# Storing the stationary operands of two GEMM stages with hi and lo side by side, and on 64 bytes

## The chip, the cores and the metric

The kernel runs on one core of one Trainium2 chip. The metric is the device time of one execution in microseconds (us); the time before is the median of three runs. The profile is of one further execution, and its times count from the start of its span. TensorE is called PE, its weight loads PEld, VectorE DVE, ScalarE ACT, GpSimd POOL and SyncE SP. L70 means line 70 of the kernel.

## What is computed

One encoder layer over 256 tokens with a model width of 2048, in float32:

```
hn   = rmsnorm(x) ; proj = hn @ w_in                      # 2048 x 18432, nine parts of 2048
o_a  = head_rmsnorm(hgrn2_bidirectional(q, v, f, lb)) * silu(z_a)          # group A
o_b  = rmsnorm(b_gate * conv3(c_gate * h_b)) * silu(z_b)                   # group B
h    = x + concat([o_a, o_b]) @ w_out                     # 4096 x 2048
gate = sigmoid(h @ w_ple_gate)                            # 2048 x 2048
h    = h + (p @ w_ple) * gate                             # p: 256 wide
out  = rmsnorm(h)
```

The change touches what `o_a` and `h` are stored as between two GEMMs, and not what is computed.

## The kernel before

**Two-part numbers.** PE takes the rounded type `float32r`. Each GEMM operand is stored as a rounded part `hi` and a rest `lo = value - hi`, and each product is made of three: hi x hi, hi x lo and lo x hi. For the weights the class `Stream` does it: SP loads 1 MB into one of three `raw` tiles, ACT rounds it into half of an `spl` tile (L69), and DVE subtracts (L70), up to three halves ahead of their use.

**Stages.** Up to about 866 us the kernel multiplies `hn` by `w_in` (`gemm_in`, lines 284 to 288), with the HGRN2 and convolution work of ACT, DVE and POOL under it. The outputs of that stage are the mixed activations. `mixa` (group A, 16 heads) is written in `finish_pair`, one head at a time: two transposes of `ogz` into PSUM, then ACT writes hi (L360) and DVE lo (L361). `mixb` (group B) is written at L587 and L588.

Then comes the output projection, four blocks of 512 columns. `gemm_tok` (lines 621 to 633) runs over the rows of the weight in steps `kt` of 128, and for each of the two token tiles m of 128 tokens it issues three matmuls:

```
pe.matmul(acc[m], lhsT=lh, rhs=w[:, k, 0, :], ...)    # L630: hi x hi
pe.matmul(acc[m], lhsT=lh, rhs=w[:, k, 1, :], ...)    # L631: hi x lo
pe.matmul(acc[m], lhsT=ll, rhs=w[:, k, 0, :], ...)    # L632: lo x hi
```

The activation is the stationary operand (`lhsT`, 128 columns, loaded anew for every matmul), the weight the moving one, 512 or 256 columns wide. Per block, `pa` sums the 16 steps of `mixa` and `pb` those of `mixb`; DVE adds each into the residual `hh`. `h_transposed` (L635 to L644) is called two and three steps later, inside the next block: PE transposes four 128x128 pieces of `hh` into one PSUM bank, and one ACT copy (L643) and one DVE subtraction (L644), each over 512 elements per partition, write `ht`.

The last stage is the gate, in blocks of 512, 512, 512, 256 and 256 columns (`GCOLS`): `gemm_tok` with `ht` as the stationary operand into `pg`, with the small product of `pt` and `w_ple` (into `pp`) ahead of each 512 columns. ACT makes the sigmoid (L679), DVE multiplies and adds, and `finish(m)` scales by the final norm and stores. The last 256 columns are made for token tile 0 and then for 1, so that `finish(0)` lies under the matmuls of tile 1. `table` (L672) loads an activation table early by a one-column activation into `dummy`.

**Where things lie.** In each partition `mixa` and `mixb` hold `[k][s][t]`: for each 128 rows k, 256 tokens of hi and then 256 tokens of lo, 4 bytes each; `ht` and `pt` likewise. A stationary load reads 128 neighbouring floats. By the program's allocation `mixa` starts at byte 196576 of a partition and `mixb`, right below it, at 163808, both 32 bytes past a multiple of 64; `ht` starts at 95232 and `pt` at 146432, both multiples of 64, as do the five `spl` tiles. The tiles of pool `ap`, below `mixa` until group A is done, are 32 bytes past a multiple of 64 too. `rx`, `rb`, `rf` and `dummy` are four tiles of two floats, in 32 bytes each.

The order of the instructions on an engine is the tile framework's, which also sets the waits; `at`/`tick` place the transposes by steps of `gemm_tok`.

Of the kernel before, what the change touches and what calls it, by code (L numbers as in the profile page):

```python
# [8 lines left out]
F32 = mybir.dt.float32  # L9
F32R = mybir.dt.float32r  # L10
U32 = mybir.dt.uint32
AF = mybir.ActivationFunctionType
ALU = mybir.AluOpType
# [4 lines left out]
P = 128  # L18
D = 2048
T = 256  # L20
NKT = D // P
NH = 16
# [58 lines left out]
def tile_hymba_encoder(  # L81
# [15 lines left out]
    act, dve, pool, pe = nc.scalar, nc.vector, nc.gpsimd, nc.tensor  # L97
    out2 = out[0].rearrange("(m p) d -> p m d", p=P)

    const = ctx.enter_context(tc.tile_pool(name="const", bufs=1))  # L100
    rawp = ctx.enter_context(tc.tile_pool(name="rawp", bufs=3))
    splp = ctx.enter_context(tc.tile_pool(name="splp", bufs=5))
    xsp = ctx.enter_context(tc.tile_pool(name="xsp", bufs=1))
# [3 lines left out]
    xp = xctx.enter_context(tc.tile_pool(name="xp", bufs=1, side="left"))  # L107
    mctx = ExitStack()
    mixp = mctx.enter_context(tc.tile_pool(name="mixp", bufs=1, side="right"))
    mixa = mixp.tile([P, NH, 2, T], F32R, name="mixa")  # L110
    actx = ExitStack()
    ap_ = actx.enter_context(tc.tile_pool(name="ap", bufs=1, side="right"))

# [10 lines left out]
    oblocks = [sum((ws.add(w_out[j, h]) for h in range(8)), []) for j in range(4)]  # L124
    gblocks, pblocks = [], []
# [48 lines left out]
    for j in range(4):  # L174
        sgn = 1 if j < 2 else -1
        pool.affine_select(
            out=tri[:, j, :], in_=tri[:, j, :], compare_op=ALU.is_ge, fill=0.0, base=0,
# [34 lines left out]
    def at(dt, fn):  # L212
        pend.append((now[0] + dt, len(pend), fn))

    def tick():
        now[0] += 1
        due = sorted(e for e in pend if e[0] <= now[0])
        for e in due:
            pend.remove(e)
        for e in due:  # L220
            e[2]()
# [9 lines left out]
            in1=xs[:, kt, 0, :], op0=ALU.mult, op1=ALU.subtract,  # L231
        )

    rx = const.tile([P, 2], F32, name="rx")
    rbc = const.tile([P, T], F32, name="rbc")
    rbc2 = const.tile([P, T], F32, name="rbc2")
    ss8 = const.tile([P, 2, 4], F32, name="ss8")
# [301 lines left out]
    mixb = None  # L539
# [7 lines left out]
    for i in range(8):  # L547
# [9 lines left out]
        for m in range(2):  # L557
            ct = 2 * i + m
            dve.tensor_scalar(cg[:, m, :], u[:, m, 0:T], cvw[:, 0, ct : ct + 1], None, op0=ALU.mult)
            for j in (1, 2):  # L560
                dve.scalar_tensor_tensor(
                    out=cg[:, m, :], in0=u[:, m, j : j + T], scalar=cvw[:, j, ct : ct + 1],
                    in1=cg[:, m, :], op0=ALU.mult, op1=ALU.add,
# [10 lines left out]
        for m in range(2):  # L574
            ct = 2 * i + m
            dve.scalar_tensor_tensor(
                out=hb[:, m, :], in0=hb[:, m, :], scalar=cnw[:, ct : ct + 1], in1=sz[:, m, :],
# [3 lines left out]
        if i == 0:  # L581
# [3 lines left out]
            mixb = bp.tile([P, NH, 2, T], F32R, name="mixb")  # L585
        hi, lo = mixb[:, 2 * i : 2 * i + 2, 0, :], mixb[:, 2 * i : 2 * i + 2, 1, :]
        act.copy(out=hi, in_=cg)  # L587
        dve.tensor_tensor(out=lo, in0=cg, in1=hi, op=ALU.subtract)  # L588

    rb = const.tile([P, 2], F32, name="rb")  # L590

    def norm_b():
        rp = psm.tile([P, 512], F32, tag="kv", name="rp")
# [16 lines left out]
    hp = ctx.enter_context(tc.tile_pool(name="hp", bufs=1, side="left", reuse_waits="tile"))  # L610
    hh = hp.tile([P, 2, D], F32, name="hh")
    nc.sync.dma_start(hh, xtok)
    ht = xsp.tile([P, NKT, 2, T], F32R, tag="act", name="ht")

    pr = hp.tile([P, 2, T], F32, name="pr")
    nc.sync.dma_start(pr, pt_in)
    pt = hp.tile([P, 2, 2, T], F32R, name="pt")
# [3 lines left out]
    def gemm_tok(acc, ids, lhs, n, ms=(0, 1)):  # L621

        kp = 1024 // n
        nk = len(ids) * kp
        for kt in range(nk):
            w = ws.get(ids[kt // kp])
            k = kt % kp
            for m in ms:
                lh, ll = lhs(kt, 0)[:, m * P : (m + 1) * P], lhs(kt, 1)[:, m * P : (m + 1) * P]
                pe.matmul(acc[m], lhsT=lh, rhs=w[:, k, 0, :], start=(kt == 0), stop=False)  # L630
                pe.matmul(acc[m], lhsT=lh, rhs=w[:, k, 1, :], start=False, stop=False)  # L631
                pe.matmul(acc[m], lhsT=ll, rhs=w[:, k, 0, :], start=False, stop=(kt == nk - 1))  # L632
            tick()

    def h_transposed(j, kk):  # L635
        tp = psm.tile([P, 512], F32, tag="tr" if kk == 0 else "kv", name=f"ht{j}_{kk}")
        for k in range(2):
            kt = 4 * j + 2 * kk + k
            for m in range(2):
                pe.transpose(tp[:, k * T + m * P : k * T + (m + 1) * P], hh[:, m, kt * P : (kt + 1) * P], ident)  # L640
        kt = 4 * j + 2 * kk
        tpv = tp.rearrange("p (k t) -> p k t", k=2)
        act.copy(out=ht[:, kt : kt + 2, 0, :], in_=tpv)  # L643
        dve.tensor_tensor(out=ht[:, kt : kt + 2, 1, :], in0=tpv, in1=ht[:, kt : kt + 2, 0, :], op=ALU.subtract)  # L644

    for j in range(4):
        cs = slice(512 * j, 512 * (j + 1))
        pa = [psg.tile([P, 512], F32, tag="g", name=f"pa{j}_{m}") for m in range(2)]
        gemm_tok(pa, oblocks[j][:8], lambda kt, s: mixa[:, kt, s, :], 512)
        for m in range(2):  # L650
            dve.tensor_tensor(out=hh[:, m, cs], in0=pa[m], in1=hh[:, m, cs], op=ALU.add)
        pb = [psg.tile([P, 512], F32, tag="g", name=f"pb{j}_{m}") for m in range(2)]
        gemm_tok(pb, oblocks[j][8:], lambda kt, s: mixb[:, kt, s, :], 512)
        for m in range(2):
            dve.scalar_tensor_tensor(
                out=hh[:, m, cs], in0=pb[m], scalar=rb[:, m : m + 1], in1=hh[:, m, cs], op0=ALU.mult, op1=ALU.add
            )
        for kk in range(2):
            at(2 + kk, lambda j=j, kk=kk: h_transposed(j, kk))
# [4 lines left out]
    fw = gp.tile([P, D], F32, name="fw")  # L664
    nc.sync.dma_start(fw, final_norm_w.rearrange("(o d) -> o d", o=1).broadcast_to([P, D]))
    ssf = const.tile([P, 2, 5], F32, name="ssf")
    rf = const.tile([P, 2], F32, name="rf")
    dummy = const.tile([P, 2], F32, name="dummy")

    def table(func, j):  # L670

# [2 lines left out]
    def gated(j, m, cs, pg, pl, last):  # L674

        n = cs.stop - cs.start
        gt = gp.tile([P, 512], F32, tag="gt", name=f"gt{j}_{m}", bufs=2)
        h = hh[:, m, cs]
        act.activation(gt[:, :n], pg, AF.Sigmoid)  # L679
        if last:  # L680
            table(AF.Sqrt, 0)
        dve.tensor_tensor(out=gt[:, :n], in0=gt[:, :n], in1=pl, op=ALU.mult)
        dve.tensor_tensor(out=h, in0=gt[:, :n], in1=h, op=ALU.add)
        if last:
            dve.scalar_tensor_tensor(
                out=gt[:, :n], in0=h, scalar=1.0, in1=h, op0=ALU.mult, op1=ALU.mult,
                accum_out=ssf[:, m, j : j + 1],
            )
        else:
            act.activation(gt[:, :n], h, AF.Square, accum_out=ssf[:, m, j : j + 1])  # L690
        pool.tensor_tensor(out=h, in0=h, in1=fw[:, cs], op=ALU.mult)  # L691

    def finish(m):
        r = rf[:, m : m + 1]
        dve.tensor_reduce(out=r, in_=ssf[:, m, :], op=ALU.add, axis=AX.X)
        act.activation(r, r, AF.Sqrt, bias=epst, scale=1.0 / D)
        if m == 0:
            table(AF.Sigmoid, 1)
        dve.reciprocal(out=r, in_=r)
        c0 = 0  # L700
        for q, n in enumerate((256, 512, 768, 512)):
            cs = slice(c0, c0 + n)
            c0 += n
            if q % 2 == 0 or m == 0:
                dve.tensor_scalar(hh[:, m, cs], hh[:, m, cs], r, None, op0=ALU.mult)
            else:
                act.mul(hh[:, m, cs], hh[:, m, cs], r)
            nc.sync.dma_start(out2[:, m, cs], hh[:, m, cs])

    for j, (c0, n) in enumerate(GCOLS):  # L710
        cs = slice(c0, c0 + n)
        if c0 % 512 == 0:
            pp = [psm.tile([P, 512], F32, tag=("o", "sc")[m], name=f"pp{j}_{m}") for m in range(2)]
            gemm_tok(pp, pblocks[c0 // 512], lambda kt, s: pt[:, kt, s, :], 512)
            pl = []
            for m in range(2):
                t = gp.tile([P, 512], F32, tag="pl", name=f"pl{j}_{m}", bufs=4)
                act.copy(out=t, in_=pp[m])
                pl.append(t)
        pg = [psg.tile([P, 512], F32, tag="g", name=f"pg{j}_{m}")[:, :n] for m in range(2)]  # L720
        po = slice(c0 % 512, c0 % 512 + n)
        if j < len(GCOLS) - 1:
            gemm_tok(pg, gblocks[j], lambda kt, s: ht[:, kt, s, :], n)
            for m in range(2):
                gated(j, m, cs, pg[m], pl[m][:, po], False)
        else:
            for m in range(2):
                gemm_tok(pg, gblocks[j], lambda kt, s: ht[:, kt, s, :], n, (m,))
                gated(j, m, cs, pg[m], pl[m][:, po], True)
                finish(m)  # L730

# [55 lines left out]
```

## Time and profile before

| | us |
|---|---|
| median of 3 runs | 1158.66 (1158.42 to 1159.83) |
| the profiled execution | 1158.74 |
| its span | 1157.0 |
| PE busy, weight loads busy | 1142.3, 981.4 |
| DVE, ACT, POOL busy | 763.6, 639.9, 234.8 |
| output projection, first matmul | at 866.3 |
| gate, first matmul of `pg` | at 1051.3 |

The span is the profiled window; the rest of the execution's time lies around it. Busy times of PE overlap from one matmul to the next, since a matmul's time runs on while the next one streams: the cost of a matmul in a row is the distance from its start to the next start, which the timeline shows, and not its duration.

### The profile page before, as it was taken

The page shows a single profiled execution, that of the slowest core. Times are in us where ns is not written, and L with a number is a line of the kernel's source. Part 1 is how long each engine was busy: PE and PEld are TensorE (multiplying, and loading weights), DVE is VectorE, ACT ScalarE, POOL GpSimd, SP SyncE. Part 2 cuts the span into 40 slices and gives each one's busy share as a digit, 9 for nine tenths or more (in the row PEclk, how much of TensorE's full clock was granted, in tenths as well). Part 3 has the DMA queues.
Part 4 walks back from the last instruction along what each step waited for, and adds up shares of the span by engine and source line. Part 5 has one row for each costly group of instructions (what it writes and reads, how often), then busy time and mean ns, then how long its engine had stood idle before and what let it go on. Part 6 is the DMA issues. An engine that isn't in the chain of part 4 may idle for free.

```text
span 1157.0 us, 16851 instructions
## 1 busy us (share of the span) xinstructions
PE 1142.3 (99%) x6832; PEld 981.4 (85%) x6832; DVE 763.6 (66%) x949; ACT 639.9 (55%) x889; POOL 234.8 (20%) x167
## 2 busy tenths in 40 slices
PE   8999999999999999999999999999999999999997
PEld 7878888888888888888888888888888888888886
DVE  6687777685958585966666666676666545545554
ACT  6767576666758584855544444444444334434554
POOL 1232414151414041331221221121210000000121
PEclk9999999999999999999999999999999999999999
DMA  8754545454544555455555555555557555555541
GB/s 284 301 175 153 183 163 196 152 183 146 198 167 159 174 177 181 152 178 182 183 187 184 198 191 187 182 182 184 187 190 262 183 198 180 191 204 196 197 166 74
DMA packets 31614, 214.29 MB, mean 185 GB/s; under 512 B 3504, under 2 KB 3888, under 8 KB 7088
## 3 DMA queue, kind: packets, MB, share of 16 engines
q1 hardware_dynamic: 31392, 213.14, 53.6%
q8 instruction: 53, 0.87, 0.3%
q14 instruction: 25, 0.20, 0.1%
q10 hardware_dynamic: 144, 0.08, 0.0%
HBM read 211.11 MB, written 2.10 MB: 184 GB/s over the span
## 4 chain that ended last, share of the span: by engine, by line
PE 93%; DVE 2%; DMA 2%; POOL 1%; ACT 1%; SPq 0%; issue 0%; ACTq 0%; DVEq 0%
PE a L288 41%; PE a L287 21%; PE a L284 3%; PE pa L630 3%; PE pb L630 3%; PE pb L631 3%; PE pb L632 3%; PE pa L631 3%; PE pa L632 3%; PE pg L630 3%; PE pg L631 3%; PE pg L632 3%; PE a L285 1%; DVE spl L70 1%; PE scps L459 1%; PE cx L501 1%
## 5 line engine op out<-in xcount | busy, mean ns | idle before, releaser
L70 DVE TENSOR_TENSOR spl<-raw,spl 128x1024 fp32r<-128x1024 f32 (+1 forms) x389 | 522.3, 1348 | 305.9 <-ACT spl L69 304.9
L288 PE MATMUL a<-xs,spl 128*128 128x512 f32 x1680 | 597.2, 398 | 0.0
L69 ACT CAST spl<-raw 128x1024 fp32r<-128x1024 f32 (+1 forms) x389 | 405.0, 1045 | 343.0 <-PE a L288 193.7
L287 PE MATMUL a<-xs,spl 128*128 128x256 f32 x1680 | 476.0, 283 | 0.5 <-DVE spl L70 0.3
L288 PEld LDWEIGHTS a<-xs,spl 128*128 128x128 f32 x1680 | 316.7, 189 | 73.0
L287 PEld LDWEIGHTS a<-xs,spl 128*128 128x128 f32 x1680 | 318.1, 189 | 3.7 <-DVE spl L70 1.3
L288 PE MATMUL a<-spl,xs 128*128 128x512 f32 x480 | 171.4, 401 | 2.2 <-DVE spl L70 2.2
L287 PE MATMUL a<-spl,xs 128*128 128x256 f32 x480 | 135.4, 282 | 0.0
L288 PEld LDWEIGHTS a<-spl,xs 128*128 128x128 f32 x480 | 91.0, 190 | 24.1 <-DVE spl L70 2.5
L287 PEld LDWEIGHTS a<-spl,xs 128*128 128x128 f32 x480 | 91.4, 190 | 0.7
L307 ACT COPY r<-a 128x256 f32<-128x256 f32 x112 | 40.6, 372 | 47.4 <-PE a L288 46.8
L691 POOL TENSOR_TENSOR hh<-hh,fw 128x512 f32<-128x512 f32 (+1 forms) x10 | 12.8, 1293 | 264.5 <-PE pp L632 245.0
L630 PE MATMUL pg<-spl,ht 128*128 128x512 f32 (+1 forms) x160 | 55.7, 348 | 0.0
L632 PE MATMUL pg<-spl,ht 128*128 128x512 f32 (+1 forms) x160 | 55.5, 347 | 0.0
L631 PE MATMUL pg<-spl,ht 128*128 128x512 f32 (+1 forms) x160 | 55.5, 347 | 0.0
L630 PE MATMUL pa<-spl,mixa 128*128 128x512 f32 x128 | 51.2, 400 | 0.0
L438 POOL TENSOR_TENSOR qc<-pf,ge 128x256 f32<-128x256 f32 x16 | 43.9, 2748 | 34.4 <-DVE pf L430 34.4
L631 PE MATMUL pb<-spl,mixb 128*128 128x512 f32 x128 | 50.6, 395 | 0.0
L630 PE MATMUL pb<-spl,mixb 128*128 128x512 f32 x128 | 50.6, 395 | 0.0
L632 PE MATMUL pb<-spl,mixb 128*128 128x512 f32 x128 | 50.6, 395 | 0.0
L631 PE MATMUL pa<-spl,mixa 128*128 128x512 f32 x128 | 50.6, 395 | 0.0
L632 PE MATMUL pa<-spl,mixa 128*128 128x512 f32 x128 | 50.6, 395 | 0.0
(174 smaller groups left out, 1233.7 us busy)
## 6 DMA issues: line engine op xcount, KB each, us to landing
raw<-in_w_in_dram SPq DMA_DIRECT2D x140, 1024.0 KB, 5.0
raw<-in_w_out_dram SPq DMA_DIRECT2D x32, 1024.0 KB, 4.9
raw<-in_w_gate_dram SPq DMA_DIRECT2D x12, 1024.0 KB, 4.9
raw<-in_w_gate_end_dram SPq DMA_DIRECT2D x4, 1024.0 KB, 4.9
raw<-in_w_in_dram SPq DMA_DIRECT2D x7, 512.0 KB, 8.4
xf<-in_xtok_dram SPq DMA_DIRECT2D x1, 2048.0 KB, 9.9
hh<-in_xtok_dram SPq DMA_DIRECT2D x1, 2048.0 KB, 8.8
raw<-in_w_ple_dram SPq DMA_DIRECT2D x4, 512.0 KB, 3.5
```

What stands on the lines that cost most here:

```text
L69: self.nc.scalar.copy(out=v[:, :, 0, :], in_=r)
L70: self.nc.vector.tensor_tensor(out=v[:, :, 1, :], in0=r, in1=v[:, :, 0, :], op=ALU.subtract)
L284: pe.matmul(a, lhsT=lh, rhs=rf, start=True, stop=False)
L285: pe.matmul(a[:, :T], lhsT=ll, rhs=rh, start=False, stop=False)
L287: pe.matmul(a[:, :T], lhsT=ll, rhs=rh, start=False, stop=False)
L288: pe.matmul(a, lhsT=lh, rhs=rf, start=False, stop=(kt == NKT - 1))
L307: act.copy(out=r, in_=acc[m][:, 1, :])
L438: pool.tensor_tensor(out=c64(dst[:, d]), in0=c64(src[:, d, :, half * P : (half + 1) * P]), in1=g.unsqueeze(3).broadcast_to([P, 2, 2, CH]), ...
L630: pe.matmul(acc[m], lhsT=lh, rhs=w[:, k, 0, :], start=(kt == 0), stop=False)
L631: pe.matmul(acc[m], lhsT=lh, rhs=w[:, k, 1, :], start=False, stop=False)
L632: pe.matmul(acc[m], lhsT=ll, rhs=w[:, k, 0, :], start=False, stop=(kt == nk - 1))
L691: pool.tensor_tensor(out=h, in0=h, in1=fw[:, cs], op=ALU.mult)
```

## The change

Four edits, and new views of the tiles in the calls of `gemm_tok`:

- `mixa` is allocated with 8 more floats per partition (32 bytes) at its end, and its view becomes `[k][t][s]`: hi and lo of one token lie side by side. The parts that ACT and DVE write and that PE loads now step by 8 bytes.
- `ht` becomes two halves. In the first (kt 0 to 7) the order is `[k][m][t][s]`, a step of 8 bytes; in the second (kt 8 to 15) it is `[k][t][m][s]`: hi and lo of token t of tile 0, then of token t of tile 1, a step of 16 bytes.
- `h_transposed` writes `ht` with one ACT copy and one DVE subtraction for each 128 rows, of 256 elements each, where it had one of each for two.
- `rx`, `rb`, `rf` and `dummy` become views of one tile `few` of 16 floats.

`mixb`, `pt` and the weights keep their order. Pools on the right side are stacked from the top down, so the longer `mixa` moves its own start, `mixb` and the tiles of `ap` 32 bytes down.

```diff
-    mixa = mixp.tile([P, NH, 2, T], F32R, name="mixa")
+    mixa = mixp.tile([P, NH * 2 * T + 8], F32R, name="mixa")[:, : NH * 2 * T]
+    mixa = mixa.rearrange("p (k t s) -> p k s t", k=NH, s=2)
...
-    rx = const.tile([P, 2], F32, name="rx")
+    few = const.tile([P, 16], F32, name="few")
+    rx, rb, rf, dummy = (few[:, 2 * j : 2 * j + 2] for j in range(4))
...
-    ht = xsp.tile([P, NKT, 2, T], F32R, tag="act", name="ht")
+    htt = xsp.tile([P, NKT * 2 * T], F32R, tag="act", name="ht")
+    htv = [htt[:, : NKT * T].rearrange("p (k m t s) -> p k s m t", k=NKT // 2, m=2, s=2),
+           htt[:, NKT * T :].rearrange("p (k t m s) -> p k s m t", k=NKT // 2, m=2, s=2)]
+    def ht(kt, s, m):
+        return htv[kt // 8][:, kt % 8, s, m, :]
...
-                lh, ll = lhs(kt, 0)[:, m * P : (m + 1) * P], lhs(kt, 1)[:, m * P : (m + 1) * P]
+                lh, ll = lhs(kt, 0, m), lhs(kt, 1, m)
...
-        tpv = tp.rearrange("p (k t) -> p k t", k=2)
-        act.copy(out=ht[:, kt : kt + 2, 0, :], in_=tpv)
-        dve.tensor_tensor(out=ht[:, kt : kt + 2, 1, :], in0=tpv, in1=ht[:, kt : kt + 2, 0, :], op=ALU.subtract)
+        for k in range(2):
+            tpv = tp[:, k * T : (k + 1) * T].rearrange("p (m t) -> p m t", m=2)
+            hi, lo = (htv[(kt + k) // 8][:, (kt + k) % 8, s] for s in range(2))
+            act.copy(out=hi, in_=tpv)
+            dve.tensor_tensor(out=lo, in0=tpv, in1=hi, op=ALU.subtract)
```

More of the change, by code (lines that the diff above doesn't have):

```diff
@@ L588, in tile_hymba_encoder @@
         dve.tensor_tensor(out=lo, in0=cg, in1=hi, op=ALU.subtract)
-    rb = const.tile([P, 2], F32, name="rb")
     def norm_b():
@@ L648, in tile_hymba_encoder @@
         pa = [psg.tile([P, 512], F32, tag="g", name=f"pa{j}_{m}") for m in range(2)]
-        gemm_tok(pa, oblocks[j][:8], lambda kt, s: mixa[:, kt, s, :], 512)
+        gemm_tok(pa, oblocks[j][:8], lambda kt, s, m: mixa[:, kt, s, m * P : (m + 1) * P], 512)
         for m in range(2):
@@ L652, in tile_hymba_encoder @@
         pb = [psg.tile([P, 512], F32, tag="g", name=f"pb{j}_{m}") for m in range(2)]
-        gemm_tok(pb, oblocks[j][8:], lambda kt, s: mixb[:, kt, s, :], 512)
+        gemm_tok(pb, oblocks[j][8:], lambda kt, s, m: mixb[:, kt, s, m * P : (m + 1) * P], 512)
         for m in range(2):
@@ L666, in tile_hymba_encoder @@
     ssf = const.tile([P, 2, 5], F32, name="ssf")
-    rf = const.tile([P, 2], F32, name="rf")
-    dummy = const.tile([P, 2], F32, name="dummy")
     def table(func, j):
@@ L713, in tile_hymba_encoder @@
             pp = [psm.tile([P, 512], F32, tag=("o", "sc")[m], name=f"pp{j}_{m}") for m in range(2)]
-            gemm_tok(pp, pblocks[c0 // 512], lambda kt, s: pt[:, kt, s, :], 512)
+            gemm_tok(pp, pblocks[c0 // 512], lambda kt, s, m: pt[:, kt, s, m * P : (m + 1) * P], 512)
             pl = []
@@ L722, in tile_hymba_encoder @@
         if j < len(GCOLS) - 1:
-            gemm_tok(pg, gblocks[j], lambda kt, s: ht[:, kt, s, :], n)
+            gemm_tok(pg, gblocks[j], ht, n)
             for m in range(2):
@@ L727, in tile_hymba_encoder @@
             for m in range(2):
-                gemm_tok(pg, gblocks[j], lambda kt, s: ht[:, kt, s, :], n, (m,))
+                gemm_tok(pg, gblocks[j], ht, n, (m,))
                 gated(j, m, cs, pg[m], pl[m][:, po], True)
```

## The prediction

> **What bounds the kernel.** I read the page, then the busy times of the two stages that use the changed tiles, then the groups by line and shape, and then the timeline of PE inside these stages.
>
> ```profile
> span 1157.0 us, 16851 instructions
> PE 1142.3 (99%) x6832; PEld 981.4 (85%) x6832; DVE 763.6 (66%) x949; ACT 639.9 (55%) x889; POOL 234.8 (20%) x167
> PE 93%; DVE 2%; DMA 2%; POOL 1%; ACT 1%; SPq 0%; issue 0%; ACTq 0%; DVEq 0%
> ```
>
> The chain that ended last is PE for 93%. In the windows of the two stages (columns: PE, PEld, DVE, ACT and POOL busy, granted clock, DMA share, GB/s):
>
> ```profile
> 866.00:1051.00 185.00, 185.00 (x810) 149.07 (x810) 98.16 (x97) 76.49 (x79) 3.59 (x2) 1.00 0.59 203
> 1054.00:1148.00 94.00, 94.00 (x506) 81.72 (x505) 51.82 (x58) 46.67 (x66) 12.05 (x9) 1.00 0.44 150
> ```
>
> PE never stops from 866 to 1148 us, at the full granted clock; DVE works about half of it, ACT and the DMAs less. So the time of these 282 us is the number of matmuls times the distance from one start to the next. The changed tiles are stationary operands of exactly these matmuls. The groups:
>
> ```profile
> L630 PE MATMUL pa<-spl,mixa 128*128 128x512 f32 x128 | 51.2, 400 | 0.0
> L631 PE MATMUL pb<-spl,mixb 128*128 128x512 f32 x128 | 50.6, 395 | 0.0
> L630 PE MATMUL pg<-spl,ht 128*128 128x512 f32 x96 | 37.6, 391 | 0.0
> L631 PE MATMUL pg<-spl,ht 128*128 128x256 f32 x64 | 18.1, 283 | 0.0
> L630 PE MATMUL pp<-spl,pt 128*128 128x512 f32 x16 | 6.2, 389 | 0.0
> ```
>
> Three lines share each group's count: 384 matmuls on `mixa`, 384 on `mixb`, 288 of 512 columns and 192 of 256 on `ht`. The same shape takes longer on `mixa` and `mixb` than on `ht` and `pt`. The timeline gives the distances (first and last of a row of matmuls: start, duration, line):
>
> ```profile
> 883.69 0.40 PE L632 MATMUL pa<-spl,mixa 128*128 128x512 f32 x1
> ...
> 886.49 0.40 PE L632 MATMUL pa<-spl,mixa 128*128 128x512 f32 x1
> ```
> ```profile
> 904.69 0.40 PE L632 MATMUL pb<-spl,mixb 128*128 128x512 f32 x1
> ...
> 908.89 0.40 PE L632 MATMUL pb<-spl,mixb 128*128 128x512 f32 x1
> ```
> ```profile
> 1119.65 0.39 PE L632 MATMUL pg<-spl,ht 128*128 128x512 f32 x1
> ...
> 1122.37 0.39 PE L632 MATMUL pg<-spl,ht 128*128 128x512 f32 x1
> ```
> ```profile
> 1129.75 0.28 PE L631 MATMUL pg<-spl,ht 128*128 128x256 f32 x1
> ...
> 1131.43 0.28 PE L630 MATMUL pg<-spl,ht 128*128 128x256 f32 x1
> ```
>
> `mixa`: 12 steps in 2.80 us, 233.3 ns each. `mixb`: 18 in 4.20, 233.3. `ht`: 12 in 2.72, 226.7, and at 256 columns 14 in 1.68, 120.0. From the last two, 256 columns stream in 106.7 ns, so 512 take 213.3, and each matmul carries a surcharge of 13.3 ns whatever its width; on `mixa` and `mixb` it is 20.0. The moving operand is `spl` in all four, the PSUM banks of `pa`, `pb` and `pg` are the same, and `pp` uses others at the pace of `pg`. What differs is the stationary tile: `mixa` and `mixb` start 32 bytes past a multiple of 64, `ht` and `pt` on one.
>
> **Part 1, the placing.** 32 bytes more in `mixa` put its start at 196576 - 32 = 196544 and `mixb`'s at 163776, both multiples of 64, and every piece in them starts a multiple of 512 or 1024 bytes further (lo in `mixa` 4 bytes past that, inside the same 64). If the 6.7 ns come from the offset, all 768 matmuls of the output projection lose them: 768 x 6.7 = 5.1 us. They lie on PE's unbroken row, so the end moves by all of it. What would be late next are the splits of the weights; with DVE at half its time they have room.
>
> **Part 2, the strided loads.** `mixa` and the first half of `ht` are loaded with a step of 8 bytes (384, and 144 + 96 matmuls), the second half of `ht` with 16 (144 + 96). Before has no strided load, so this is bounded from both sides.
>
> ```profile
> 1052.76 0.60 PE L640 MATMUL ht<-ident,hh 128*128 128x128 f32 x4
> ```
> ```profile
> L640 PE MATMUL ht<-ident,hh 128*128 128x128 f32 x32 | 4.8, 272 | 0.0
> ```
> ```profile
> L631 PEld LDWEIGHTS pa<-spl,mixa 128*128 128x128 f32 x128 | 24.0, 188 | 5.5
> L631 PEld LDWEIGHTS pg<-spl,ht 128*128 128x128 f32 x160 | 30.3, 190 | 3.6
> ```
>
> In the four transposes the streams are short and the loads set the pace: (0.60 - 0.27) / 3 = 0.109 us per load. That leaves a load 0.118 us of slack under 512 columns and 0.011 under 256. The load's own row is no longer off the 64 bytes (188 against 190), so what the offset costs is paid by the stream, not by the load. From below: the surcharge of all 864 strided matmuls could vanish, 864 x 13.3 = 11.5 us less. From above: a load that reads each element from a place of its own could take two or more times 0.109, or disturb the stream in proportion to the bytes it passes over; the rivals price both. I take zero: the nearest rows, loads of 128 elements with a dense step, are hidden at both widths.
>
> The Trainium skill, page SBUF — State Buffer, section Specifications, states that SBUF has 16-byte lines, that a read needs at least two hits on a line for full bandwidth, and that each crossing to a new line costs. By it the step of 8 bytes (two floats of a line) is free and the step of 16 (one) is not, which speaks against the second half of `ht`; no row of before has such a load, and the third case below is what it would do here.
>
> **Part 3, the writes.**
>
> ```profile
> L643 ACT CAST ht<-ht 128x512 fp32r<-128x512 f32 x8 | 4.7, 587 | 2.4 <-PE ht L640 2.4
> L644 DVE TENSOR_TENSOR ht<-ht,ht 128x512 fp32r<-128x512 f32 x8 | 5.5, 689 | 1.5 <-ACT ht L643 1.5
> L307 ACT COPY r<-a 128x256 f32<-128x256 f32 x112 | 40.6, 372 | 47.4 <-PE a L288 46.8
> L308 DVE TENSOR_TENSOR hb<-a,r 128x256 f32<-128x256 f32 x48 | 18.5, 423 | 13.8 <-ACT r L307 13.8
> L360 ACT ACTIVATE mixa<-ogt,vec 128x256 fp32r<-128x256 f32 x16 | 7.5, 469 | 0.0
> L361 DVE SCALAR_TENSOR_TENSOR mixa<-ogt,vec,mixa 128x256 fp32r<-128x256 f32 x16 | 7.6, 478 | 0.0
> ```
>
> The 8 copies and 8 subtractions of `ht` become 16 of half the length: ACT 16 x 372 - 8 x 587 = 1.3 us more, DVE 16 x 423 - 8 x 689 = 1.3 us more, in 185 us in which DVE is free for 87. The last four pieces are the ones that could be late: their transposes end at 1053.4, and kt 12 of the gate's first block comes 72 matmuls of 226.7 ns, 16 us, after the block's start at 1051.3. That covers four operations of under 0.5 us, and would cover them at double length. Without that cover the last chain of four would cost 0.8 us. The 16 + 16 writes of `mixa` keep their number; if a step of 8 bytes doubled them, ACT and DVE would each have 7.6 us more, spread over eight pairs under `gemm_in`. I put that at zero, with 1 us as the upper bound, since DVE is busy for 474 of 660 us there:
>
> ```profile
> 40.00:700.00 660.00, 657.31 (x4369) 572.46 (x4368) 474.00 (x612) 409.29 (x594) 183.99 (x115) 1.00 0.52 177
> ```
>
> **Part 4, one tile for four.**
>
> ```profile
> 1150.30 0.20 ACT L672 ACTIVATE dummy<-epst 128x1 f32<-128x1 f32 x1
> 1150.41 0.16 DVE L695 TENSOR_REDUCE rf<-ssf 128x1 f32<-128x5 f32 x1
> ```
>
> If the framework takes `few` as one thing, the reduction into `rf` must wait for the activation into `dummy`, which ends at 1150.50. Behind it on DVE stands the reciprocal, and the last stores wait for that: 0.1 to 0.2 us at the end. In `finish(0)` the reciprocal would wait 1.5 us for the next table, under the matmuls of tile 1. Zero to 0.2 us; I take 0.
>
> **The sum** against the profiled execution: 1158.74 - 5.1 = 1153.6. The median of the runs shown is 0.08 lower, so 1153.5.
>
> **The rivals.**
> *The strided loads disturb the stream less.* The surcharge depends on how the load's bytes lie (13.3 against 20.0 ns), so another pattern can also lower it. Against it: no row shows less than 13.3 in these stages. At half the surcharge 864 x 6.7 = 5.8 us more is gained, 1147.8; at none, 1142.0.
> The Trainium skill, page TensorE: Matmul & The Clock Gate, section Back-to-back issue gap, gives N / 2.4 + 2.5 ns for a single matmul, 215.8 at 512 columns; the trace shows 226.7, so the measurement decides for dense loads, and by the page's figure as an estimate the strided stages would end near 1144.
>
> *Slower: loads with a step of 16 bytes set the pace at 256 columns.* Place: the 96 matmuls of kt 8 to 15 in the last two blocks. A load twice as long takes 0.218 us, hidden under 226.7 at 512 columns but not under 120.0: 96 x 0.098 = 9.4 us, 1162.9. It decides from 0.120 + 5.1 / 96 = 0.173 us per load on. For it: only 0.011 us of slack there. Against it: nothing shows that a load's time depends on its step.
>
> *Slower: the surcharge grows with the bytes passed over*, 1024 and 2048 in place of 512: 26.7 and 53.3 ns. `mixa` gains nothing and loses 384 x 6.7 = 2.6 us, `mixb` gains 2.6, `ht` loses 240 x 13.3 + 240 x 40 = 12.8: 1171.5. For it: an offset of 32 bytes alone costs half as much again. Against it: one more piece in nine should cost a ninth, not a half.
>
> *The change doesn't do what it says:* the 6.7 ns belong to the place of `mixa` and `mixb` at the top of the memory, not to 64 bytes, and strides cost nothing: 1158.7.
>
> **How the numbers follow.** Forecast 0.34; less disturbance 0.26; long loads 0.16; bytes passed over 0.15; no effect 0.09. The first two are faster, 0.60; the next two slower, 0.31; the last the same, 0.09. 0.2% is 2.3 us, about what a measurement of this kernel can tell from no change. The range goes from the second case's end, 1142, over the long loads to half of the fourth case (surcharges grown half as far, 1165) with the 1 and 0.2 us of parts 3 and 4 and a little for loads over twice as long: 1167. It leaves out most of the fourth case. For the faster cases alone it is 1142 to 1156.
>
> **What would show it.** Right: in the profile after, distances of 226.7 ns on `mixa` and `mixb`, with 226.7 and 120.0 on `ht` in both halves, the gate as long as before and the projection 5 us shorter. Wrong: 233 on `mixb` (the offset isn't the cause); distances on `mixa` or `ht` below 220 (second case); about 0.2 us at 256 columns for kt 8 to 15 alone, with longer PEld rows there (third); distances that grow by step, 240 and 267, at both widths (fourth). DVE or ACT as a releaser of PE after 866 us would say that part 3 was mispriced.

## The result and the profile after

| | before | after |
|---|---|---|
| median, us | 1159.24 (4 runs) | 1167.69 (4 runs) |
| ratio to before | | 1.0072, 95% interval 1.0059 to 1.0084 |
| profiled span, us | 1157.0 | 1165.5 |

The kernel became slower by 8.4 us, where 5.1 us less were forecast. One execution of a kernel below, the profiled one of e2, took 1879.19 us at a granted clock of 0.556; it does not count in that kernel's ratio, and its profile is not used. The page of after, first lines and chain:

```profile
span 1165.5 us, 16875 instructions
PE 1151.2 (99%) x6832; PEld 1001.9 (86%) x6832; DVE 767.6 (66%) x957; ACT 643.2 (55%) x897; POOL 234.9 (20%) x167
PE 93%; DVE 2%; DMA 2%; POOL 1%; ACT 1%; issue 0%; SPq 0%; ACTq 0%; DVEq 0%
```

PE is still the chain, and no wait of PE is recorded from 866 us to the end of its matmuls. The span grew by 8.5 us and the busy time of PEld by 20.5. The groups by line and shape of after (busy us, mean ns; L639 to L641 are before's L630 to L632):

```profile
L640 PE MATMUL pa<-spl,mixa 128*128 128x512 f32 x128 | 50.4, 394 | 0.0
L640 PE MATMUL pb<-spl,mixb 128*128 128x512 f32 x128 | 49.8, 389 | 0.0
L640 PEld LDWEIGHTS pg<-spl,ht 128*128 128x128 f32 x160 | 41.0, 256 | 1.8
L640 PE MATMUL pg<-spl,ht 128*128 128x512 f32 x96 | 38.0, 396 | 0.0
L640 PEld LDWEIGHTS pa<-spl,mixa 128*128 128x128 f32 x128 | 24.7, 193 | 4.9
L640 PEld LDWEIGHTS pb<-spl,mixb 128*128 128x128 f32 x128 | 24.0, 188 | 5.1
L640 PE MATMUL pg<-spl,ht 128*128 128x256 f32 x64 | 21.7, 340 | 0.0
```

The loads of `ht` went from 190 to 256 ns on average, those of `mixa` from 188 to 193. The timeline of PE in after: `mixa`, `mixb`, the last two gate blocks' kt 0 to 7, and their kt 8 to 15 (first and last of 16, 20, 17 and 15 matmuls in a row):

```profile
879.76 0.39 PE L640 MATMUL pa<-spl,mixa 128*128 128x512 f32 x1
...
883.26 0.39 PE L640 MATMUL pa<-spl,mixa 128*128 128x512 f32 x1
...
899.67 0.39 PE L640 MATMUL pb<-spl,mixb 128*128 128x512 f32 x1
...
903.98 0.39 PE L641 MATMUL pb<-spl,mixb 128*128 128x512 f32 x1
...
1124.76 0.28 PE L640 MATMUL pg<-spl,ht 128*128 128x256 f32 x1
...
1126.68 0.28 PE L641 MATMUL pg<-spl,ht 128*128 128x256 f32 x1
...
1133.73 0.40 PE L640 MATMUL pg<-spl,ht 128*128 128x256 f32 x1
...
1137.00 0.40 PE L639 MATMUL pg<-spl,ht 128*128 128x256 f32 x1
```

A load of `ht` in the row of 8 bytes, and one in the row of 16:

```profile
1125.12 0.20 PEld L641 LDWEIGHTS pg<-spl,ht 128*128 128x128 f32 x1
...
1134.06 0.33 PEld L639 LDWEIGHTS pg<-spl,ht 128*128 128x128 f32 x1
```

Start to start: `mixa` 3.50 / 15 = 233.3 ns, `mixb` 4.31 / 19 = 226.8, the step of 8 bytes at 256 columns 1.92 / 16 = 120.0, the step of 16 bytes 3.27 / 14 = 233.6. Under 512 columns of the gate the mean distances, over all matmuls of a kind, are 234.0 at the step of 8 and 235.0 at 16, against 226.8 in before. The windows of the last two gate blocks, from their first matmul's start to the last one's, before and then after (PE, PEld, DVE, ACT, POOL busy, clock, DMA, GB/s):

```profile
1125.32:1148.23 22.91, 22.91 (x192) 22.91 (x191) 11.40 (x20) 11.13 (x22) 5.49 (x5) 1.00 0.06 21
```
```profile
1122.84:1156.52 33.68, 33.68 (x192) 33.67 (x191) 11.43 (x19) 11.15 (x22) 5.49 (x5) 1.00 0.09 32
```

The clock is full in both, DVE, ACT and POOL do the same work, and 192 matmuls take 10.8 us more. By stages, from the starts of their first matmuls, after against before: the first stage 2.3 us less, the output projection 182.5 against 185.0, the gate's 512 columns 76.3 against 74.0, its 256 columns 10.8 more, the tail 0.2 more; together 8.5. The first stage's share is no part of the change that can be told: kernels below with the same first stage began the projection at 867.5 (e3) and 868.6 us (e10), after at 864.0.

### The profile page after: what moved, and what is told of

Read it like the earlier page. It is cut to its first block, busy times and chain, and to the rows that moved or that the text cites. A ratio compares the mean times of both kernels' runs of the same rounds, so it can differ in the third digit from the quotient of the medians.

```text
span 1165.5 us, 16875 instructions
## 1 busy us (share of the span) xinstructions
PE 1151.2 (99%) x6832; PEld 1001.9 (86%) x6832; DVE 767.6 (66%) x957; ACT 643.2 (55%) x897; POOL 234.9 (20%) x167
## 4 chain that ended last, share of the span: by engine, by line
PE 93%; DVE 2%; DMA 2%; POOL 1%; ACT 1%; issue 0%; SPq 0%; ACTq 0%; DVEq 0%
PE a L292 40%; PE a L291 20%; PE pg L639 3%; PE pg L640 3%; PE pg L641 3%; PE a L288 3%; PE pa L639 3%; PE pa L640 3%; PE pa L641 3%; PE pb L639 2%; PE pb L641 2%; PE pb L640 2%; PE a L289 1%; DMA raw<-in_w_in_dram 1%; DVE spl L70 1%; PE scps L463 1%
## 5 line engine op out<-in xcount | busy, mean ns | idle before, releaser
L639 PE MATMUL pg<-spl,ht 128*128 128x512 f32 (+1 forms) x160 | 60.0, 375 | 0.0
L641 PE MATMUL pg<-spl,ht 128*128 128x512 f32 (+1 forms) x160 | 59.8, 374 | 0.0
L640 PE MATMUL pg<-spl,ht 128*128 128x512 f32 (+1 forms) x160 | 59.8, 373 | 0.0
L639 PE MATMUL pa<-spl,mixa 128*128 128x512 f32 x128 | 51.1, 399 | 0.0
L641 PE MATMUL pa<-spl,mixa 128*128 128x512 f32 x128 | 50.4, 394 | 0.0
L639 PE MATMUL pb<-spl,mixb 128*128 128x512 f32 x128 | 49.8, 389 | 0.0
L641 PE MATMUL pb<-spl,mixb 128*128 128x512 f32 x128 | 49.8, 389 | 0.0
L640 PE MATMUL pb<-spl,mixb 128*128 128x512 f32 x128 | 49.8, 389 | 0.0
```

## The experiments

Three theories stood at the start. The one from the trace, **L**: the step of a stationary load and its offset from 64 bytes set its cost. The rivals: **W**, the gate is late because `ht` is written in more and strided pieces; and **P**, which came up over the 64 bytes: in after, `few` moved the `spl` tiles by 64 bytes too, so `mixb` may have gained by its distance from the moving operand and not by its place. I count this phase as the start of the stationary tile less that of `spl`, modulo 256: in before `mixa` and `mixb` are at 224 and `ht` and `pt` at 0; in after all are at 0.

**e1: the placing alone.** Before with

```diff
-    mixa = mixp.tile([P, NH, 2, T], F32R, name="mixa")
+    mixa = mixp.tile([P, NH * 2 * T + 8], F32R, name="mixa")[:, : NH * 2 * T]
+    mixa = mixa.rearrange("p (k s t) -> p k s t", k=NH, s=2)
```

> Before with the 32 bytes more in mixa alone: mixa and mixb on a multiple of 64, all loads dense, ht, the writes and the four small tiles as before. Theory L (what a stationary load costs is set by its step and its offset from 64 bytes): 226.7 ns on mixa and on mixb, 768 x 6.7 = 5.1 us less, about 1154.1 us, gate as before. Rival P (the offset matters against the moving operand's place within 256 bytes, and mixb came down to 226.7 because spl moved by 64 bytes too): here mixa and mixb lie 192 bytes from spl's phase, so 230 to 233 ns stay, 1157 to 1159 us.

Measured: 1154.74 us (5 runs), 0.9953 of before (0.9939 to 0.9967). The time alone is L's, 0.6 us from it. The timeline of `mixa` (15 matmuls in a row) is not:

```profile
879.74 0.39 PE L633 MATMUL pa<-spl,mixa 128*128 128x512 f32 x1
...
882.94 0.39 PE L632 MATMUL pa<-spl,mixa 128*128 128x512 f32 x1
```

3.20 / 14 = 228.6 ns; over all matmuls the distances on `mixa` and `mixb` are 229.0 and 228.9 ns, between the two theories' numbers. They are worth 3.3 us in the projection (181.7 against 185.0 us); the rest of the gain lies outside it. Lying on 64 bytes is not enough for 226.7.

**e2: a step of 8 bytes in both halves of `ht`.** After with

```diff
-           htt[:, NKT * T :].rearrange("p (k t m s) -> p k s m t", k=NKT // 2, m=2, s=2)]
+           htt[:, NKT * T :].rearrange("p (k m t s) -> p k s m t", k=NKT // 2, m=2, s=2)]
```

> After with the second half of ht stored like the first (step of 8 bytes in place of 16). Theory L: the 96 matmuls of 256 columns go from 233 to 120 ns, 10.9 us less; under 512 columns 235 to 234, 0.1 us; about 1156.7 us. Rival W (the strided writes and the doubled copies of ht make the gate late): the copies stay 16 + 16, so most of the loss stays, 1162 us or more, and PE shows waits for ACT or DVE in the gate.

Measured: 1157.75 us (11 runs), 0.9984 of before (0.9975 to 0.9994). That is 1 us over L's number and 4 us under W's least; the 16 + 16 copies are still there, so W falls.

**e3: a step of 16 bytes in both halves.** The opposite edit, in the first half of `htv`.

> After with the first half of ht stored like the second (step of 16 bytes throughout). Theory L: another 96 matmuls of 256 columns go from 120 to 233 ns, 10.9 us more, and 144 of 512 from 234 to 235, 0.1 us: about 1178.7 us. Rival W (writes): eight more pieces are written at the longer step, at most 8 x 0.3 us on ACT and DVE, beside other work: 1167.7 to 1170 us.

Measured: 1181.28 us (4 runs), 1.0183 (1.0169 to 1.0197): 13.6 us over after, where L had 11.0 and W at most 2.3. The window of the two blocks in e3:

```profile
1126.61:1171.07 44.46, 44.46 (x193) 44.46 (x192) 11.51 (x19) 11.14 (x22) 5.42 (x5) 1.00 0.07 24
```

They take 10.8 us more than in after, L's price to 0.1. The rest of the difference lies ahead of the projection, which began at 867.5 us here and at 864.0 in after.

**e4: four phases in one kernel.** All loads dense, `few` kept; the longer tiles put `mixa` at phase 192 and `mixb` at 128, and the pad puts `pt` at 64:

```diff
+    mixa = mixp.tile([P, NH * 2 * T + 24], F32R, name="mixa")[:, : NH * 2 * T]
...
+            mixb = bp.tile([P, NH * 2 * T + 16], F32R, name="mixb")[:, : NH * 2 * T]
...
+    hp.tile([P, 16], F32, name="pad")
```

> All loads dense, few kept, and four places: against spl's phase within 256 bytes mixa lies at 192, mixb at 128, pt at 64 and ht at 0, all on multiples of 64. Theory L: 226.7 ns on all four, about 1154.1 us. Rival P: the distances differ between mixa, mixb, pt and ht, by steps of some 3 to 7 ns, 1150 to 1159 us.

Measured: 1157.09 us (10 runs), 0.9975 (0.9966 to 0.9984). The timeline of PE in e4, `mixa` and then `mixb` (14 matmuls in a row each):

```profile
879.71 0.39 PE L633 MATMUL pa<-spl,mixa 128*128 128x512 f32 x1
...
882.68 0.39 PE L634 MATMUL pa<-spl,mixa 128*128 128x512 f32 x1
...
902.62 0.40 PE L633 MATMUL pb<-spl,mixb 128*128 128x512 f32 x1
...
905.66 0.39 PE L634 MATMUL pb<-spl,mixb 128*128 128x512 f32 x1
```

2.97 / 13 = 228.5 ns here, 3.04 / 13 = 233.8 there; over all matmuls 229.1 on `mixa` and 232.6 on `mixb`, 233.4 on `pt` and 227.1 on `ht`. All four lie on multiples of 64. L's rule of 64 bytes falls; `mixa` has in e4 the phase and the distance that it had in e1, at another place.

**e5: all dense, all at phase 0.** e4 with 8 floats in place of 24 and without the other two pads.

> All loads dense, few kept and mixa 32 bytes longer: every stationary tile of the output projection and the gate has spl's phase within 256 bytes. Theory P (the surcharge is set by the distance of the stationary from the moving operand within 256 bytes): 226.7 ns on mixa and mixb, 768 x 6.7 = 5.1 us under before, 1154.4 us, the gate as before. Rival L (a multiple of 64 bytes is enough): the same here; the two part in the kernels with other phases.

Measured: 1153.05 us (5 runs), 0.9939 (0.9927 to 0.9952): faster than before and, by 14.6 us, than after. The groups of e5:

```profile
L632 PE MATMUL pa<-spl,mixa 128*128 128x512 f32 x128 | 49.9, 390 | 0.0
L632 PE MATMUL pb<-spl,mixb 128*128 128x512 f32 x128 | 49.8, 389 | 0.0
```

Start to start 227.2 and 226.7 ns: what the forecast gave to the output projection is there when no load is strided. The projection takes 180.1 us against 185.0 in before; the rest of the gain lies ahead of it, where the profiled executions scatter.

**e6: `mixa` with a step of 8 at phase 192, `mixb` with a step of 16 at phase 0, `ht` dense.** `mixb` is also written in twice as many pieces.

```diff
+    mixa = mixp.tile([P, NH * 2 * T + 24], F32R, name="mixa")[:, : NH * 2 * T]
...
+            mixb = bp.tile([P, NH * 2 * T + 48], F32R, name="mixb")[:, : NH * 2 * T]
+            mixb = mixb.rearrange("p (k t m s) -> p k s m t", k=NH, m=2, s=2)
```

> mixa with a step of 8 bytes at 192 bytes from spl's phase, mixb with a step of 16 bytes at 0, ht dense at 0. The claim that a load with a step of 16 bytes takes 0.233 us of its own: mixb at 233 to 238 ns under 512 columns, the gate's 256 columns back at 120.0. Theory P: mixa's distance differs from the 233.3 that the step of 8 has at phase 0. Rival (a step of 8 costs 20 ns whatever the phase): mixa stays at 233.3. About 1160 us.

Measured: 1158.32 us (one run; before 1159.83). From the groups of e6, by line and shape:

```profile
L635 PE MATMUL pb<-spl,mixb 128*128 128x512 f32 x128 | 50.9, 398 | 0.0
...
L635 PEld LDWEIGHTS pb<-spl,mixb 128*128 128x128 f32 x128 | 39.6, 310 | 0.0
...
L635 PE MATMUL pg<-spl,ht 128*128 128x256 f32 x64 | 18.1, 283 | 0.0
```

`mixb` runs at 235.0 ns with loads of 310 on the row, next to no idle time between them, and the dense gate at 120.0 again: the step, and not the stage, makes the load long. `mixa` stays at 233.4 at phase 192, as at phase 0 in after: for a step of 8, P had it wrong and the rival right, as far as two phases tell.

**e7 and e8: the first stage at another phase.** e5 with `xs` 16 and 32 floats further into its tile (64 and 128 bytes), `ht` in place; its tile is as much longer, which moves `pt` to phases 64 and 128:

```diff
+    xs = xsp.tile([P, NKT * 2 * T + 16], F32R, tag="act", name="xs")[:, 16 :]
...
```

> As the dense kernel with all phases at 0, but xs moved 64 bytes against spl, so that the 4608 matmuls of the first stage run at another phase; ht stays at 0. Theory P: the 353 ns of a pair of 512 and 256 columns change by 3 to 12 ns, the time by 7 to 28 us, either way. Rival (phase matters only where every matmul has the same width): the first stage stays within 2 us.

> The same with xs moved by 128 bytes. Theory P: another change of the pair of 512 and 256 columns by 3 to 12 ns, 7 to 28 us either way. Rival (phase matters only where every matmul has the same width): the first stage stays within 2 us.

Measured: 1151.42 us (4 runs), 0.9926 (0.9912 to 0.9939), and 1152.15 us (4 runs), 0.9927 (0.9912 to 0.9942): no difference from e5 that the intervals hold. From its first matmul to the first of the projection, the first stage took 857.1 us in e5, 857.1 in e7 and 857.5 in e8. Between matmuls of 512 and 256 columns in turn the distances shift (with `xs` moving, 234.1 and 119.2 ns in e5, 230.6 and 122.6 in e8), but hardly their sum. P, which had at least 7 us, failed there; an effect of one or two us could not be told, since kernels with the same first stage took up to 862.1 us for it (e10). `pt` followed P: 233.5 ns at phase 64 (e7) and 233.0 at 128 (e8).

**e9: fine phases.** e5 with `mixa` at phase 16, `mixb` at 32 and `pt` at 240, by views that start 4, 8 and 60 floats into longer tiles.

> All loads dense; against spl's phase mixa lies at 16 bytes, mixb at 32, pt at 240, ht at 0. Theory P, with 0 as the best phase: mixa, mixb and pt all above 226.7 ns, up to 233. Rival (only the offset from 64 bytes counts, and in steps of 32): mixa and pt, whose first 64 bytes are cut by a quarter, at 226.7 or 233.3 like the two known cases. About 1153 to 1158 us.

Measured: 1157.74 us (one run; before 1159.55). `mixa` 233.1, `mixb` 233.3, `pt` 227.1 ns. `pt` starts 48 bytes past a multiple of 64 and loses 0.4 ns: I had expected more of phase 240.

**e10: e2's kernel again, for its profile.**

> The kernel with a step of 8 bytes in both halves of ht once more, for its profile. Theory (the load with a step of 8 bytes keeps the dense pace, and only disturbs the stream): 120 ns at 256 columns and 233 to 234 at 512 in both halves, the gate's last two blocks 22.9 us long as before. Rival (the loss at 256 columns comes with the split copies): these blocks stay longer than before. About 1157.8 us.

Measured: 1160.76 us (one run; before 1159.55), 3 us over e2's median; the projection began late in it, at 868.6 us. The question was the last blocks. The timeline of their second half in e10 (16 matmuls in a row):

```profile
1132.79 0.28 PE L640 MATMUL pg<-spl,ht 128*128 128x256 f32 x1
...
1134.59 0.28 PE L640 MATMUL pg<-spl,ht 128*128 128x256 f32 x1
```

1.80 / 15 = 120.0 ns, and both blocks took 22.92 us: at 256 columns the step of 8 costs nothing. Under 512 it is 233.9 and 234.1 ns in the two halves.

**e11: the period.** e5 with `mixb` 256 bytes short of a multiple of 1024 from `spl`, `pt` 256 past one, and `mixa` 16 short.

> All loads dense. Against spl, counted in multiples of 1024 bytes and the rest: mixa lies 16 bytes short of a multiple, mixb 256 short, pt 256 past one, ht on one. Theory P with a period of 256 bytes: mixb and pt at 226.7 ns like phase 0, mixa near the 227.1 that pt had at 240. Rival with a period of 512: mixb and pt differ from 226.7, and mixa's value is a new one. Rival L (64 bytes alone): mixb and pt at 226.7, mixa at 230 or more. About 1153 to 1157 us.

Measured: 1151.71 us (one run; before 1160.75). The timeline of e11 (13 matmuls in a row):

```profile
900.64 0.39 PE L634 MATMUL pb<-spl,mixb 128*128 128x512 f32 x1
...
903.36 0.39 PE L634 MATMUL pb<-spl,mixb 128*128 128x512 f32 x1
```

2.72 / 12 = 226.7 ns on `mixb`; over all matmuls 226.7 on `pt` and 227.6 on `mixa`, which is at phase 240 and 48 bytes past a multiple of 64. A period of 256 bytes fits all kernels, and the rule of 64 bytes fails a second time.

All dense loads under 512 columns, mean distance from start to start by phase:

| phase | 0 | 16 | 32 | 64 | 128 | 192 | 224 | 240 |
|---|---|---|---|---|---|---|---|---|
| ns | 226.6 to 227.2 | 233.1 | 233.3 | 233.4, 233.5 | 232.6, 233.0 | 228.9 to 229.1 | 233.3 | 227.1, 227.6 |

Left out is `pt` right behind strided loads of `ht`: in after the first five distances of such a row go up to 236, and the others are 226 and 227.

## Why the prediction was wrong

**What bounds the kernel** held: PE's unbroken row, and nothing else late.

**Part 1, the placing.** Half of its 5.1 us came: `mixb` fell to 226.8 ns, 384 x 6.6 = 2.5 us. For `mixa` the step of 8 took back what the phase gave. The cause was named wrongly: with `mixb` on 64 bytes but at phase 192 the gain is 4.4 ns (e1), and with `mixa` 16 bytes short of phase 0 and off the 64 bytes it is nearly whole (e11). The rows of before held only phases 0 and 224, so they could not tell the two apart; `few`, which I treated as a matter of waits, is what brought `spl` to the same phase.

**Part 2, the strided loads**, is the step that failed: "I take zero: the nearest rows, loads of 128 elements with a dense step, are hidden at both widths." A load with a step of 16 bytes sets a pace of 233 ns, twice the 109 of the dense one, and under 256 columns, which stream at 120.0, nothing hides the rest: 96 x 113.6 = 10.9 us, measured 10.8. That is the rival of long loads with its place and mechanism; its 9.4 us was low since a dense load was doubled (0.218) and 0.233 came. e2, e3, e6 and e10 show the step as the cause, by undoing it, by doubling it and by moving it to another stage. The claim against it, that nothing shows a load's time to depend on its step, was an absence of rows and no evidence, and the slack of 0.011 us spoke for the rival. Why a load at the step of 16 takes this long was not measured.

The same zero was wrong under 512 columns too, where both steps cost the stream: 384 x 6.6 = 2.5 us on `mixa`, which ate its gain of part 1, and 2.3 us in the gate. With these terms the profiled execution is accounted for: 1153.6 + 10.8 + 2.5 + 2.3 + 0.2 in the tail, less 2.3 in the first stage, is 1167.1; it took 1167.2. That the time ended so near the range's end is in part luck, since no term foresaw these 2.3 us of the first stage.

The Trainium skill's rule of two hits on a 16-byte line (page SBUF — State Buffer, section Specifications) gave the order rightly: at 256 columns the step of 8 is free (120.0) and the step of 16 is not (233.6). Under 512 columns the step of 8 is not free, 234.0 against 226.8. By the Trainium skill, page TensorE: Matmul & The Clock Gate, section LDWEIGHTS, a load's time goes by its columns alone; here 128 columns take 233 ns at the step of 16, so the measurement decides.

**The bytes passed over**: in part. A surcharge of 20 ns at the step of 8 under 512 columns against 13.3 dense is half of the growth that this rival had, and none of it shows at 256 columns, where the rival had the same growth (its signs of 240 and 267 ns hold for 512 columns; at 256 its terms give 133 and 160).

**Part 3, the writes.** Each piece of `ht` was priced at 372 and 423 ns. From the trace of after, by the tile `ht` (duration min/median/max):

```profile
L654 ACT CAST ht<-ht x16: 392/514/682, 912.2 to 1051.1; 128x256 fp32r<-128x256 f32 x16
L655 DVE TENSOR_TENSOR ht<-ht,ht x16: 418/514/644, 913.5 to 1052.4; 128x256 fp32r<-128x256 f32 x16
```

Some take up to 682 and 644 ns, but they were covered as said: no wait of PE. The long ones are those at the step of 16: the median on ACT and DVE is 395 and 426 ns in e10, where all pieces have the step of 8, and 627 and 623 in e3, where all have 16. The writes of `mixa` take 490 and 477 against 469 and 478.

**Part 4, one tile for four.** The end of DVE's chain in after, with the activation of ACT beside it:

```profile
1158.70 0.08 DVE L694 DVE_READ_ACCUMULATOR gt<-hh 128x1 f32 x1
1158.71 0.20 ACT L681 ACTIVATE few<-epst 128x1 f32<-128x1 f32 x1
1158.82 0.16 DVE L704 TENSOR_REDUCE few<-ssf 128x1 f32<-128x5 f32 x1
```

The reduction follows the accumulator at 0.12 us, as in before (1150.29 and 1150.41), and starts ahead of the activation's end at 1158.91: no wait was added.

**The range** ended at 1167.0 since the case of the bytes passed over was taken in only half; the time lay 0.7 us above it. The long loads alone would have stayed inside, at 1164.4, had the whole gain of part 1 come.

## What to carry to other kernels

Before a stationary operand is stored with a stride, look up the narrowest matmul that loads it: a load has only that matmul's time to hide in, and at a step of 16 bytes it took twice as long. Where matmuls run back to back, compare the start-to-start distance, not the duration, between tiles at different addresses; a few nanoseconds on 768 matmuls were 4.9 us of the output projection here (e5). When two tiles differ in pace, note all addresses involved, the moving operand's too, before naming the alignment of one of them as the cause.

## What the runs showed of the hardware

- The distance of matmuls with dense loads under 512 columns depends on the difference of the two operands' addresses modulo 256: 226.7 ns at 0 and up to 233.5 at 16, 32, 64 and 224; in before the clock was at full in the windows of both (0 and 224). The Trainium skill, page TensorE: Matmul & The Clock Gate, section Step-by-step: what each phase is for, says that loading the next weights takes no read bandwidth from the running matmul; these distances, which depend on the addresses alone, are not in line with that. What the two reads collide in, if they do, was not measured.
- In the first stage, where widths of 512 and 256 alternate, no phase tried (`xs` 0, 64 and 128 bytes past that of `spl`) changed its length beyond 0.4 us.
- A load of 128 floats sets a pace of 109 ns dense (the transposes of before), is hidden under 120 at a step of 8 bytes, and sets a pace of 233 at 16. No step between or above was tried.
- Writes from PSUM of 256 floats per partition took 395 ns on ACT and 426 on DVE at a step of 8 bytes (e10), 627 and 623 at 16 (e3).
